# Two of sixteen gate projections computed as seven Strassen products inside the values' stage of a decoder layer, with the other gates dealt out anew

## The chip, the cores and the metric

The kernel runs on one core of a Trainium2 chip. The metric is device time in microseconds (us) for one launch. A version's time is the median of its runs; before the change there are three. Besides these one execution was profiled, and every view of the trace here comes from it.

The engines are named as the profile names them: PE is TensorE (matmuls), PEld its weight loads, DVE is VectorE, ACT is ScalarE, POOL is GpSimd, and SP is SyncE, which here does nothing but start DMAs. Each takes its instructions strictly in order; a wait at the head of an engine's list holds all that stands behind it.

## The reference

One layer, 1024 tokens, model width 1024, all in float32. What matters here is the first projection and where its columns go:

```python
h = rms_norm(x, pre_mix_g[l])
proj = h @ w_in[l]
qa, ka, va, qb, kb, vb, gates = jnp.split(proj, split_at, axis=-1)
...
g_a, g_b = jnp.split(jax.nn.sigmoid(gates), 2, axis=-1)
mix = (g_a * ya + g_b * yb) @ w_mix_out[l]
x = x + rms_norm(mix, post_mix_g[l])
...
y = (jax.nn.gelu(gate, approximate=True) * val) @ w_down[l]
x = x + rms_norm(y, post_ffn_g[l])
```

`ya` comes from a differential attention of four heads (A), `yb` from three groups of four dilated window heads (B), merged by their log-sum-exps. The values `va` and `vb` are together 2048 columns of `proj`, the gates another 2048, which is sixteen tiles of 128 columns.

## The kernel before

**Products.** A float32 product is made of three passes over operands that were split into a rounded high part and a rest: high by high, low by high, high by low (`mm3`, L153 to 157). One product step is therefore three matmuls with a 128x128 stationary and a 128x512 moving operand. A weight tile of 128x512 reaches this form in three moves: SP starts its load into a tile `raw` (`load_raw`, L126), ACT writes the high part `whi` (L149), DVE subtracts to get the low part `wlo` (L146).

**Stages.** The stages follow one another on PE without a gap in the program: the values' stage (up to about 162 us into the span), the four heads of attention A, the twelve heads of attention B, the two output products with the gates (`branch`, from L1178), the mix, then the up and down products of the MLP.

**The values' stage** (L467 to 667) computes the 2048 value columns by Strassen's scheme: halves of the tokens, of the 1024 rows of the weight and of the columns make 2x2 blocks, and seven products `p1` to `p7` replace eight. There are two such sets (`i` = 0 and 1), each product has four steps (`k`), and each step is 12 matmuls into four PSUM banks. `steps_v` lists the 56 steps by hand. All that a step needs is made ahead of it:

- `fetch_v` loads the weight tiles, 8 to 10 steps ahead; `p5` and `p7` need two tiles each. The loads go round robin through six `raw` tiles, and from L646 on also through pieces of tiles of the rotary tables that have served their turn (`more_tags`).
- `ready_v`, up to 5 steps ahead, forms sums of weight tiles on DVE (`wz`, all by the helper `tt` at L345) and splits the result.
- `step_v` runs the matmuls; at a product's last step `take_v` moves the four banks into the result tiles `yv`: some are copied by ACT, some added by DVE. This is traced at a high priority (`tc.high_priority`).
- `put_v` multiplies finished tiles by the norm's factor on DVE (L550) and stores them to the buffer `v_d` in HBM, by DMAs that POOL starts (L551). `STORE_AT` says at which steps this is done for the first set.

Into the same steps are woven the sums of squares of the norm, `angles` and `make_sines` (the rotary tables, L354 to 368 and L425), `turn_norms` (the norm's factors turned by eight PE transposes into a row `rstd_row`, L428 to 435) and `scale_tables` (tables times that row, by L383 and L345, and three stores to `tab_d` by POOL, L444).

**A gate** (`proj_t` with `put_gate`, L234 to 253) is a tile of 128 gate columns by 1024 tokens: two weight loads of 128x512, two splits, 16 product steps (48 matmuls with two halves of tokens), and per half a DVE product with `rstd_row` and a store to `gt_d`, which ACT's queue starts. The gates depend on nothing but `h`, so they serve as filler: `START_GATES` run right behind the values' stage, `A_FILLS` says for each head of attention A which pieces are spread between its blocks (`g` a gate, `p` the next head's projections, `P` the first projection of B, `v` and `x` loads of values, `w` and `V` their splits), and `B_GATES` run in the last head of B. `proj_b` and `split_b` do the same for B's projections and values.

**Order.** A scheduler orders each engine's instructions from the traced program, its priorities, and a model of the engines' timing; only what is marked by `behind_marks` or `issue_after` is tied to a place. The order of a program is fixed when it is built. Where the text speaks of what stands where, it means this fixed order.

Of the kernel before, what the change touches and what calls it, by code (L numbers as in the profile page):

```python
# [43 lines left out]
FULL = 2  # L44


NH = NF // 2
AHEAD, T1_AT, LAST = 4, 5, 7
MIX_UNITS = {3: (0,), 4: (1,), 5: (2, 4), 6: (5,), 7: (6, 3, 7)}
START_GATES, A_FILLS, B_GATES = 1, ("gpgg", "gpvgg", "wgpgg", "xgPVgg"), 3  # L50
SLOTS = 18
LEFT_PAD = 48


XT_BUFS, NORM_AT, ANGLES_AT, SINES_AT, TABLES_AT, STORE_AT = 6, 14, 25, 33, 34, {35: 0, 36: 3, 39: 2, 41: 1}

K_FIRST = (4, 0, 5, 1, 6, 2, 7, 3)
RSQRT_MAGIC = float(0x5F3759DF)
# [29 lines left out]
def trunk(ctx: ExitStack, tc: tile.TileContext, a, out):  # L88
# [372 lines left out]
    with ExitStack() as st_y:  # L461
# [6 lines left out]
        def turns(pattern, *ps):  # L468

            ks = [iter(range(4)) for _ in ps]  # L470
            return [(ps[c], 1, next(ks[c])) for c in pattern]

        steps_v += [("p1", 1, k) for k in range(4)] + turns((0, 0, 1, 0, 1, 0, 1, 1), "p5", "p6")
        steps_v += turns((0, 0, 1, 1, 1, 1, 0, 0), "p3", "p7") + [("p4", 1, k) for k in range(4)]
        wz = [t[:, k % 2] for t in [wv.tile([P, 2, 512], F32, tag=f"wz{i}", name="wz") for i in range(2)] for k in range(2)]
        ready, got_v = {}, {}
# [10 lines left out]
        def new_y(name, pool=None):  # L487
            return [(pool or yv).tile([P, 512], F32, tag=f"y{name}{m}", name="yv") for m in range(4)]

        def fetch_v(n):  # L490
            p, i, k = steps_v[n]
            which = {"p1": ((0, 0),), "p2": ((0, 1),), "p5": ((1, 0), (1, 1)), "p6": ((0, 0),), "p7": ((0, 0), (1, 0)),
                     "p4": ((1, 1),), "p3": ((0, 1),)}[p]
            got_v[n] = [load_raw(a["w_v"][j * 4 + k][:, (2 * i + c) * 512 : (2 * i + c + 1) * 512], next(tags), parts=1 if n else 2)
                        for c, j in which]

        def ready_v(n, w=512):
            p, _, k = steps_v[n]
# [54 lines left out]
        quarter = {(0, i): new_y(f"a{i}") for i in range(2)}  # L553
        banks = {}

        def step_v(n):
            p, i, k = steps_v[n]
            x = xs_of[p]
            if p in ("p1", "p2", "p5") and k == 0:
                left = p == "p1"  # L560
                banks[left] = ([psum() for _ in range(3)] + [psum(F32, ps_o, "o")] if left else
                               [psum(F32, q, t) for q, t in ((ps_s, "s"), (pt, "pt")) for _ in range(2)])
            use = banks[p in ("p1", "p6", "p7", "p4")]
            wh, wl = ready.pop(n)
            for m in range(4):
                tk = slice(m * P, (m + 1) * P)
                mm3(use[m], x[0][:, k, tk], x[1][:, k, tk], wh, wl, k == 0 and p in ("p1", "p2", "p5"), k == 3, p in ("p6", "p7", "p4", "p3"))
            if k < 3:
                return
            with tc.high_priority(offset=80):  # L570
                for m in range(4):
                    take_v(p, i, m, use[m])
            if p == "p7" and i == 0:
                for m in range(4):
                    tt(quarter[3, 0][m], banks[False][m], quarter[3, 0][m], ALU.add)
# [56 lines left out]
        for n in range(8, len(steps_v)):  # L632
            p, i, k = steps_v[n]
            while fetched < min(n + (8 if n <= TABLES_AT else 10), len(steps_v)):
                fetch_v(fetched)
                fetched += 1
            while made < min(n + 5, len(steps_v)):
                ready_v(made)
                made += 1
            if 0 <= n - NORM_AT < 11:  # L640
                norm_x(n - NORM_AT)
            if n == NORM_AT + 11:
                lambda_scale()
            if n == TABLES_AT + 2:
                scale_tables(*args)
            if n == TABLES_AT + 4:  # L646
                tags = more_tags()
            if n == ANGLES_AT:
                pos = [load_raw(a["positions"][sl].partition_broadcast(P), next(tags)) for sl in halves()]
                args = [tb.tile([P, S], F32, tag=n_, name=n_) for n_ in ("sin", "cos")]  # L650
                angles(pos, *args, tb)
            if n in STORE_AT:
                put_v(STORE_AT[n], 0, True)
            if n == SINES_AT:
                make_sines(*args)
            if n == TABLES_AT:
                turn_norms()
            if k == 0 and (p, i) in places_y:
                q, name, pool = places_y[p, i]
                quarter[q, i] = new_y(name, pool)  # L660
            step_v(n)
            if k == 3 and i and p in ("p1", "p7", "p4", "p3"):
                put_v({"p1": 0, "p7": 3, "p4": 2, "p3": 1}[p], 1, p == "p1")
            if (p, i) == ("p5", 1):

                again.append(load_raw(a["xT"][k][:, 512:], next(tags)))
            if (p, i) == ("p6", 1):
                with behind_marks():
                    split_x(k, halves()[1], again[k])
# [18 lines left out]
    def split_values(vs, res):  # L688

        with behind_marks():  # L690
            for v in vs:
                res.append(v_tiles())
                split(*res[-1], v)
# [175 lines left out]
        later(1, sums)  # L869
        later(3, norm)  # L870

    free_gates = list(range(2 * KC))

    def gates(n):

# [6 lines left out]

    tabs_b, wk_b = [], []

    def proj_b(g, h, res, between=None):
        dil = DIL[g]
        qh, ql, kh, kl = (slot(n) for n in ("qh", "ql", "kh", "kl"))
        res += [qh, ql, kh, kl]
        n = 512 // dil

        def put(hi, lo):
            def evacuate(half, sl, ps):
                t = rotated(ps, *tabs_b, sl, 64).rearrange("p (i r) -> p r i", r=dil)
                o, l = (t_.rearrange("p (r i) -> p r i", r=dil)[:, :, half * n : (half + 1) * n] for t_ in (hi, lo))
                nc.scalar.activation(o, t, AF.Copy)
                nc.vector.tensor_tensor(l, t, o.bitcast(F32), op=ALU.subtract)
            return evacuate

        yield from proj_t(QB + g * 512 + h * P, put(qh, ql))
        if between:  # L900
            between()
        yield from proj_t(KB + g * 512 + h * P, put(kh, kl))
# [12 lines left out]
    def fetch_b(pair, g):  # L915
        got_b[pair, g] = fetch_values(DIL[g], 512 + g * 512 + pair * 256)

    def split_b(pair, g):
        split_values(got_b.pop((pair, g)), vs_b[pair, g])

    def a_weight(i):

# [220 lines left out]
    for n, (pair, g, h) in enumerate(steps[:-1]):  # L1143
        sbs = []
        todo = [functools.partial(attend_b, g, h, jj, ops_b[pair, g, h], vs_b[pair, g], sbs) for jj in range(4)]
        nxt = steps[n + 1]
        if h % 2:
            fetch_b(*nxt[:2])
        fill = proj_b(nxt[1], nxt[2], ops_b[nxt], functools.partial(split_b, *nxt[:2]) if h % 2 else None)
        interleave(jobs(todo), 4, (itertools.chain(fill, once(load_ots)) if nxt == steps[-1] else fill, 8))  # L1150
        if pair == 1 and g < 2 and h == 2:
            for i, fn in zip((0, 2, 3, 6, 9), merge(g)):
                later(i, fn, 0)
# [648 lines left out]
```

## Time and profile before

| what | value |
|---|---|
| median of three runs | 1684.5 us (1682.96, 1684.5, 1685.84) |
| the profiled execution's own time | 1684.85 us |
| its span in the trace | 1683.1 us |
| time outside the span | 1.75 us |
| mean granted clock of PE | 0.999 |
| PE busy in the span | 1668.5 us, 99% |
| DVE busy | 1308.4 us, 78% |
| ACT busy | 913.4 us, 54% |
| POOL busy | 170.2 us, 10% |
| DMA | 241.59 MB, mean 144 GB/s |

Busy time counts an instruction from its start to its end; matmuls overlap, so a PE that is 99% busy has hardly a moment in which none runs, and its time is the number of matmuls times the distance of two starts, plus the waits. A row of a timeline gives the start, the duration, the engine, the line, the operation, output and inputs with their shapes, and how many such instructions in a row it sums up; in brackets stands idle time before it and what ended it. Tile names in views of the trace are without buffer numbers.

### The profile page before, as it was taken

How to read it: one execution, taken by the hardware profiler on the slowest of the kernel's cores; microseconds unless marked ns; L12 is line 12 of the kernel's file. 1: busy time of each engine (PE TensorE's matmuls, PEld its weight loads, DVE VectorE, ACT ScalarE, POOL GpSimd, SP SyncE). 2: the span in 40 equal slices, each digit the busy share in tenths (PEclk: the TensorE clock that was granted, in tenths of full speed). 3: DMA queues.
4: the chain of work that ended last, by engine and by line, in shares of the span. 5: the costliest groups of instructions: out<-in, count | busy, mean ns of one | idle time of the engine just before them, and what ended most of it. 6: DMA issues, size and time to landing. Idle time of an engine off the chain costs nothing. (4 is left out here: it accounts for less than half of the span.)

```text
span 1683.1 us, 22937 instructions
## 1 busy us (share of the span) xinstructions
PE 1668.5 (99%) x7878; PEld 1394.0 (83%) x7878; DVE 1308.4 (78%) x2430; ACT 913.4 (54%) x1707; POOL 170.2 (10%) x267
## 2 busy tenths in 40 slices
PE   9999999999999999999999999999999999999997
PEld 7888888888888888888888888887888888888886
DVE  8795576877777777788766865988888778799978
ACT  7633574655445677667554533565554455255453
POOL 0031000000000000000123400022211121000000
PEclk9999999999999999999999999999999999999999
DMA  8767421315122212343676532267755655296524
GB/s 269 234 221 266 132 83 62 107 57 147 48 70 75 76 57 78 107 135 105 212 264 223 188 113 89 58 159 172 161 133 132 156 137 126 96 348 214 193 88 150
DMA packets 117253, 241.59 MB, mean 144 GB/s; under 512 B 14528, under 2 KB 23680, under 8 KB 117136
## 3 DMA queue, kind: packets, MB, share of 16 engines
q1 hardware_dynamic: 89296, 171.28, 30.6%
q0 software_dynamic: 23088, 60.45, 15.2%
q10 hardware_dynamic: 4752, 8.39, 1.3%
q8 instruction: 62, 1.02, 0.3%
q14 instruction: 55, 0.45, 0.1%
HBM read 177.54 MB, written 47.86 MB: 134 GB/s over the span
## 5 line engine op out<-in xcount | busy, mean ns | idle before, releaser
L157 PE MATMUL acc<-xl,whi 128*128 128x512 f32 x768 | 302.5, 394 | 0.0
L155 PE MATMUL acc<-xh,whi 128*128 128x512 f32 x768 | 302.0, 393 | 0.0
L156 PE MATMUL acc<-xh,wlo 128*128 128x512 f32 x768 | 301.7, 393 | 0.0
L149 ACT ACTIVATE whi<-raw 128x512 fp32r<-128x512 f32 (+1 forms) x249 | 154.1, 627 | 180.6 <-PE acc L157 115.4
L146 DVE TENSOR_TENSOR wlo<-raw,whi 128x512 fp32r<-128x512 f32 (+1 forms) x249 | 172.2, 700 | 32.8 <-ACT whi L149 27.9
L156 PEld LDWEIGHTS acc<-xh,wlo 128*128 128x128 f32 x768 | 144.4, 188 | 27.9
L157 PEld LDWEIGHTS acc<-xl,whi 128*128 128x128 f32 x768 | 144.4, 188 | 27.7
L155 PEld LDWEIGHTS acc<-xh,whi 128*128 128x128 f32 x768 | 144.5, 188 | 27.3
L155 PE MATMUL acc<-mh,whi 128*128 128x512 f32 x384 | 149.7, 390 | 1.7 <-ACT u L1447 1.3
L156 PE MATMUL acc<-mh,wlo 128*128 128x512 f32 x384 | 149.4, 389 | 0.0
L157 PE MATMUL acc<-ml,whi 128*128 128x512 f32 x384 | 149.1, 389 | 0.0
L700 ACT ACTIVATE t<-acc 64x512 f32<-64x512 f32 (+1 forms) x160 | 94.7, 592 | 62.0 <-PE acc L157 60.4
L149 ACT ACTIVATE whi<-s 128x512 fp32r<-128x512 f32 x80 | 49.8, 627 | 90.7 <-PE acc L157 63.5
L1443 DVE TENSOR_TENSOR u<-acc,u 128x512 f32<-128x512 f32 x100 | 68.5, 687 | 29.1 <-PE acc L157 28.9
L701 DVE TENSOR_TENSOR t<-acc,cos 128x512 f32<-128x512 f32 x64 | 44.2, 690 | 55.4 <-ACT t L700 51.9
L155 PEld LDWEIGHTS acc<-mh,whi 128*128 128x128 f32 x384 | 72.1, 188 | 17.7 <-ACT u L1447 2.2
L157 PEld LDWEIGHTS acc<-ml,whi 128*128 128x128 f32 x384 | 72.1, 188 | 14.9
L156 PEld LDWEIGHTS acc<-mh,wlo 128*128 128x128 f32 x384 | 72.1, 188 | 14.9
L1620 PE MATMUL acc<-whi,wlo 128*128 128x512 f32 x216 | 76.1, 390 | 0.0
L1619 PE MATMUL acc<-whi 128*128 128x512 f32 x216 | 74.8, 389 | 0.0
L1621 PE MATMUL acc<-wlo,whi 128*128 128x512 f32 x216 | 71.6, 390 | 0.0
L787 DVE CUSTOM_DVE_ANT_0 s<-s,mask_a 128x512 f32<-128x512 f32 (+3 forms) x96 | 52.5, 555 | 23.2 <-PE s L785 18.5
(402 smaller groups left out, 4015.2 us busy)
## 6 DMA issues: line engine op xcount, KB each, us to landing
raw<-in_w_in SPq DMA_DIRECT2D x96, 256.0 KB, 2.8
raw<-in_w_v SPq DMA_DIRECT2D x71, 256.0 KB, 4.6
raw<-in_w_up SPq DMA_DIRECT2D x68, 256.0 KB, 3.6
raw<-c_d SPq DMA_DIRECT2D x48, 256.0 KB, 3.6
c_d<-c SPq DMA_DIRECT2D x22, 512.0 KB, 4.0
s<-in_w_up POOLq DMA_DIRECT2D x40, 256.0 KB, 4.2
s<-s POOLq DMA_DIRECT2D x40, 256.0 KB, 3.9
raw<-in_w_down SPq DMA_DIRECT2D x37, 256.0 KB, 3.5
```

The lines of the kernel that those rows point to most:

```text
L146: eng.tensor_tensor(lo, src, hi.bitcast(F32), op=ALU.subtract)
L149: copy = nc.scalar.activation(hi, src, AF.Copy)
L155: nc.tensor.matmul(o, sh, mh, start=first, stop=False, skip_group_check=on)
L156: nc.tensor.matmul(o, sl, mh, start=False, stop=False, skip_group_check=on)
L157: nc.tensor.matmul(o, sh, ml, start=False, stop=last, skip_group_check=on)
L700: nc.scalar.activation(t1[dst], ps[src], AF.Copy)
L701: nc.vector.tensor_tensor(t2, ps, cos[:, sl], op=ALU.mult)
L787: nc.vector.tensor_tensor_reduce(out=s_sb[:, c0:c1], in0=ps, in1=mask, scale=-scale, scalar=3.0e38, op0=ALU.add, op1=ALU.min, accum_out=mx ...
L1443: nc.vector.tensor_tensor(to, made(p), x, op=ALU.add)
L1619: nc.tensor.matmul(banks[m], gh[:, tk], wh, start=f == 0, stop=False)
L1620: nc.tensor.matmul(banks[m], gl[:, tk], wh, start=False, stop=False)
L1621: nc.tensor.matmul(banks[m], gh[:, tk], wl, start=False, stop=f == NH - 1)
```

## The change

With `PAIRS = 1`, gates 14 and 15 are no longer computed as plain gates. The two form one more Strassen set within the values' stage: two gates by two halves of the tokens by two halves of the rows of the weight. Each of the seven products is one step of 12 matmuls into one PSUM bank. The seven steps stand among those of the second set's `p1` (`steps_v` has 63 now). The gate's weights are taken in the four 128x512 blocks of `w_in`; `fetch_v` loads nine tiles for them, since `p5` and `p7` take two each, and they go through the same `raw` tiles and `wz` sums.

- `step_gate` runs a step. The left bank is one tile of pool `pt` and takes `p1`, then `p6`, `p7` and `p4` on top; the right bank is one tile of `s` and takes `p2`, `p5`, `p3`.
- `take_gate` moves the sums between products: `p2`, `p6` and `p7` are copied by ACT into four `yv` tiles, `p1`, `p7` and `p3` are followed by a DVE addition that reads a bank, and each finished tile is multiplied by `rstd_row` on DVE and stored to `gt_d` by POOL.
- The four `yv` tiles are those which the first set's `p2`/`p1` and `p5`/`p7` results had (names `a0` and `b3`), once these were stored.
- Steps of gates are made ready 4 steps ahead instead of 5; `more_tags` begins four steps later; `STORE_AT` has other steps.

Of the fourteen plain gates none runs at the start now, 2, 3, 3 and 4 run in the four heads of attention A (3 each before), and 2 run in the last head of B (3 before). The loads and splits of values have other places among the fills. In attention B, `split_b` is done in two pieces, ahead of the next head's first projection and between the two, and `fetch_b` comes one head earlier. `NH` keeps its value.

On PE the two gates were 96 matmuls and are 84. Elsewhere the change removes for them 4 loads, 4 ACT splits, 4 DVE subtractions, 4 DVE products and 4 stores from ACT's queue; it adds 9 loads on SP, 7 ACT splits, 3 ACT copies, 7 DVE subtractions, 4 DVE sums of weights, 3 DVE additions, 4 DVE products and 4 stores from POOL.

```diff
-START_GATES, A_FILLS, B_GATES = 1, ("gpgg", "gpvgg", "wgpgg", "xgPVgg"), 3
+PAIRS, START_GATES, A_FILLS, B_GATES = 1, 0, ("gpg", "gpvggw", "gpxggV", "gPggg"), 2
-XT_BUFS, ..., STORE_AT = 6, 14, 25, 33, 34, {35: 0, 36: 3, 39: 2, 41: 1}
+XT_BUFS, ..., STORE_AT = 6, 14, 25, 33, 34, {32: 0, 37: 3, 42: 2, 46: 1}
...
-        steps_v += [("p1", 1, k) for k in range(4)] + turns((0, 0, 1, 0, 1, 0, 1, 1), "p5", "p6")
+        gate_steps = [(p, "gate", 0) for p in ("p2", "p1", "p5", "p6", "p7", "p4", "p3")]
+        own = [("p1", 1, k) for k in range(4)]
+        steps_v += [*own[:2], *gate_steps[:4], own[2], gate_steps[4], own[3], *gate_steps[5:]]
+        steps_v += turns((0, 0, 1, 0, 1, 0, 1, 1), "p5", "p6")
...
+        def take_gate(p, n, use):
+            def put(q):
+                sl = halves()[q % 2]
+                y = gate_y[n][q]
+                tt(y, use if p == "p4" else y, rstd_row[:, sl], ALU.mult)
+                nc.gpsimd.dma_start(gt_d[gate_of(n, q // 2)][:, sl], y)
+            y = gate_y[n]
+            if p in ("p2", "p6", "p7"):
+                nc.scalar.activation(y[{"p2": 0, "p6": 1, "p7": 3}[p]], use, AF.Copy)
+            if p == "p1":
+                tt(y[0], use, y[0], ALU.add)
+                put(0)
+            if p == "p7":
+                tt(y[3], banks[n, False], y[3], ALU.add)
+                put(3)
+            if p == "p4":
+                put(2)
+            if p == "p3":
+                tt(y[1], use, y[1], ALU.add)
+                put(1)
+
+        def step_gate(p, n, wh, wl):
+            left = p in ("p1", "p6", "p7", "p4")
+            if p in ("p1", "p2"):
+                banks[n, left] = psum(F32, pt, "pt") if left else psum(F32, ps_s, "s")
+            x, use = xs_of[p], banks[n, left]
+            for k in range(4):
+                c = slice(k * P, (k + 1) * P)
+                mm3(use, wh[:, c], wl[:, c], x[0][:, k], x[1][:, k], k == 0 and p in ("p1", "p2", "p5"), k == 3, ...)
+            with tc.high_priority(offset=80):
+                take_gate(p, n, use)
...
-            while made < min(n + 5, len(steps_v)):
+            while made < min(n + (4 if i == 'gate' else 5), len(steps_v)):
...
-            if n == TABLES_AT + 4:
+            if n == TABLES_AT + 8:
                 tags = more_tags()
...
+            if (p, i, k) == ("p2", "gate", 0):
+                ya, yb = new_y("a0"), new_y("b3", yw)
+                gate_y.update({x: {0: ya[x], 1: ya[2 + x], 3: yb[x], 2: yb[2 + x]} for x in range(PAIRS)})
...
-    free_gates = list(range(2 * KC))
+    free_gates = list(range(2 * (KC - PAIRS)))
...
-    def split_b(pair, g):
-        split_values(got_b.pop((pair, g)), vs_b[pair, g])
+    def split_b(pair, g, n=2):
+        vs = got_b[pair, g]
+        split_values([vs.pop(0) for _ in range(n)], vs_b[pair, g])
...
-        if h % 2:
-            fetch_b(*nxt[:2])
-        fill = proj_b(nxt[1], nxt[2], ops_b[nxt], functools.partial(split_b, *nxt[:2]) if h % 2 else None)
+        if h % 2 == 0 and n + 2 < len(steps):
+            fetch_b(*steps[n + 2][:2])
+        fill = proj_b(nxt[1], nxt[2], ops_b[nxt], *([functools.partial(split_b, *nxt[:2], 1)] * 2 if h % 2 else ()))
```

More of the change, by code (lines that the diff above doesn't have):

```diff
@@ L44 @@
 FULL = 2
-NH = NF // 2
+NH = (NF + 0) // 2
 AHEAD, T1_AT, LAST = 4, 5, 7
 MIX_UNITS = {3: (0,), 4: (1,), 5: (2, 4), 6: (5,), 7: (6, 3, 7)}
-START_GATES, A_FILLS, B_GATES = 1, ("gpgg", "gpvgg", "wgpgg", "xgPVgg"), 3
+PAIRS, START_GATES, A_FILLS, B_GATES = 1, 0, ("gpg", "gpvggw", "gpxggV", "gPggg"), 2
 SLOTS = 18
 LEFT_PAD = 48
-XT_BUFS, NORM_AT, ANGLES_AT, SINES_AT, TABLES_AT, STORE_AT = 6, 14, 25, 33, 34, {35: 0, 36: 3, 39: 2, 41: 1}
+XT_BUFS, NORM_AT, ANGLES_AT, SINES_AT, TABLES_AT, STORE_AT = 6, 14, 25, 33, 34, {32: 0, 37: 3, 42: 2, 46: 1}
 K_FIRST = (4, 0, 5, 1, 6, 2, 7, 3)
@@ L488, in new_y, with gate_of @@
             return [(pool or yv).tile([P, 512], F32, tag=f"y{name}{m}", name="yv") for m in range(4)]
+        def gate_of(x, c):
+            return 2 * (KC - PAIRS + x) + c
         def fetch_v(n):
@@ L493, in fetch_v @@
                      "p4": ((1, 1),), "p3": ((0, 1),)}[p]
-            got_v[n] = [load_raw(a["w_v"][j * 4 + k][:, (2 * i + c) * 512 : (2 * i + c + 1) * 512], next(tags), parts=1 if n else 2)
-                        for c, j in which]
+            if i == "gate":
+                srcs = [w_in[where[GT + gate_of(k, c) * P]][:, j * 512 : (j + 1) * 512] for c, j in which]
+            else:
+                srcs = [a["w_v"][j * 4 + k][:, (2 * i + c) * 512 : (2 * i + c + 1) * 512] for c, j in which]
+            got_v[n] = [load_raw(src, next(tags), parts=1 if n else 2) for src in srcs]
         def ready_v(n, w=512):
@@ L554, in trunk @@
         banks = {}
+        gate_y = {}
+        def take_gate(p, n, use):
[25 more added lines that the diff above has]
+                c = slice(k * P, (k + 1) * P)
+                mm3(use, wh[:, c], wl[:, c], x[0][:, k], x[1][:, k], k == 0 and p in ("p1", "p2", "p5"), k == 3, p in ("p6", "p7", "p4", "p3"))
+            with tc.high_priority(offset=80):
+                take_gate(p, n, use)
         def step_v(n):
             p, i, k = steps_v[n]
+            if i == "gate":
+                step_gate(p, k, *ready.pop(n))
+                return
             x = xs_of[p]
@@ L883, in trunk, with proj_b @@
     tabs_b, wk_b = [], []
-    def proj_b(g, h, res, between=None):
+    def proj_b(g, h, res, ahead=None, between=None):
         dil = DIL[g]
@@ L897, in put @@
             return evacuate
+        if ahead:
+            ahead()
         yield from proj_t(QB + g * 512 + h * P, put(qh, ql))
```

## The prediction

> **What bounds the kernel now.** I read the busy shares first, then the waits of PE, then the stage that the change touches, slice by slice.
>
> ```profile
> span 1683.1 us, 22937 instructions
> PE 1668.5 (99%) x7878; PEld 1394.0 (83%) x7878; DVE 1308.4 (78%) x2430; ACT 913.4 (54%) x1707; POOL 170.2 (10%) x267
> ```
> ```profile
> PE acc L155 <- ACT xh L387: 1.4, 1, 1.4
> PE acc L155 <- DVE ya L1211: 1.4, 2, 0.9
> PE acc L155 <- ACT u L1447: 1.3, 1, 1.3
> PE pt L594 <- DVE t4l L591: 1.2, 1, 1.2
> PE acc L155 <- ACT mh L149: 0.3, 1, 0.3
> PE acc L156 <- DVE xl L383: 0.2, 1, 0.2
> ```
>
> PE is the bound: all its waits (total, times, longest) come to 5.8 us. Fewer matmuls shorten the span, as long as nothing makes PE wait. In the stage that takes the new products the second engine is not idle either:
>
> ```profile
> 80.00:90.00 10.00, 10.00 (x46) 8.29 (x45) 10.00 (x20) 6.34 (x10) 0.00 (x0) 1.00 0.14 46
> 90.00:100.00 10.00, 10.00 (x46) 8.29 (x45) 10.00 (x20) 2.42 (x4) 0.00 (x0) 1.00 0.79 229
> 100.00:110.00 10.00, 10.00 (x50) 8.38 (x49) 9.67 (x20) 4.12 (x6) 2.66 (x1) 1.00 0.56 190
> 110.00:120.00 10.00, 10.00 (x45) 8.25 (x44) 10.00 (x21) 1.90 (x4) 8.80 (x14) 1.00 0.79 277
> 120.00:130.00 10.00, 10.00 (x45) 8.27 (x45) 9.02 (x16) 5.84 (x10) 5.04 (x9) 1.00 1.03 380
> 130.00:140.00 10.00, 10.00 (x46) 8.26 (x45) 4.67 (x7) 3.58 (x6) 0.00 (x0) 1.00 0.96 334
> ```
>
> The columns are the stretch and its length, then PE, PEld, DVE, ACT and POOL busy, PE's clock, the share of the DMA engines and GB/s. From 80 to 120 us DVE is full (39.67 of 40), and from 120 to 140 the DMA engines are. The seven new steps stand just there. PE does not wait in it before: what DVE does late there, nobody needs soon.
>
> **The saving.** PE's price is the distance of two starts. The second set's first `p1` step begins at 95.55; the matmul at 108.69 is the 58th after it:
>
> ```profile
> 95.55 0.39 PE L155 MATMUL acc<-whi,xh 128*128 128x512 f32 x1
> ...
> 108.69 0.40 PE L156 MATMUL pt<-whi,xl 128*128 128x512 f32 x1
> 108.93 1.04 PE L434 MATMUL s<-ident,rstd_row 128*128 128x128 f32 x8
> 109.72 0.47 PE L157 MATMUL pt<-wlo,xh 128*128 128x512 f32 x1
> ```
>
> So 13.14 / 58 = 0.2266 us each, and the eight transposes 0.79. Two gates take 84 matmuls for 96: 12 x 0.2266 = **2.72 us saved**. That is all there is to gain on PE, and every other edit can only move waits.
>
> **The first new wait: PE at the gate's `p6`.** In DVE's order after the change, this is what stands between the last weight split of the second set's `p1` (`wlo_1205`) and the addition that reads the gate's left bank `pt_1155` with `p1` in it:
>
> ```order
> L146 TENSOR_TENSOR wlo_1205<-raw_1083,whi_1204 128x512
> L146 TENSOR_TENSOR wlo_1232<-raw_1104,whi_1231 128x512
> L383 SCALAR_TENSOR_TENSOR neg_1178<-sin_899,rstd_row_112 128x512
> L345 TENSOR_TENSOR cos_900<-cos_900,rstd_row_112 128x512
> L383 SCALAR_TENSOR_TENSOR neg_1178<-sin_899,rstd_row_112 128x512
> L345 TENSOR_TENSOR cos_900<-cos_900,rstd_row_112 128x512
> L146 TENSOR_TENSOR wlo_1237<-wz_135,whi_1236 128x512
> L345 TENSOR_TENSOR sin_899<-sin_899,rstd_row_112 128x512
> L345 TENSOR_TENSOR yv_141<-acc_1067,yv_141 128x512
> L345 TENSOR_TENSOR yv_142<-acc_1068,yv_142 128x512
> L345 TENSOR_TENSOR yv_143<-acc_1069,yv_143 128x512
> L345 TENSOR_TENSOR yv_1119<-pt_1155,yv_1119 128x512
> ```
>
> Before, the additions for `p1` stood behind the store's products, and the tables came later:
>
> ```order
> L550 TENSOR_SCALAR yv_475<-yv_475,edge_58 128x512
> L550 TENSOR_SCALAR yv_476<-yv_476,edge_58 128x512
> L345 TENSOR_TENSOR yv_141<-acc_1061,yv_141 128x512
> L146 TENSOR_TENSOR wlo_1179<-wz_135,whi_1178 128x512
> L345 TENSOR_TENSOR yv_142<-acc_1062,yv_142 128x512
> L345 TENSOR_TENSOR yv_143<-acc_1063,yv_143 128x512
> ```
>
> What moved: the gate's addition is behind 16 store products instead of 12 and five operations on tables. PE's order there after the change (`pt_1155` and `s_1127` are the gate's banks, `wlo_1205` its own step's weight):
>
> ```order
> L157 MATMUL o_1070<-wlo_1205,xh_98 128x512
> L155 MATMUL s_1127<-xh_98,whi_1055 128x512
> ...
> L155 MATMUL pt_1155<-t2h_116,whi_1086 128x512
> ...
> L155 MATMUL s_1370<-whi_1275,xh_98 128x512
> ...
> L155 MATMUL pt_1155<-t3h_118,whi_1174 128x512
> ...
> L157 MATMUL s_1370<-wlo_1276,xh_98 128x512
> ```
>
> These are the starts of the gate's `p5`, of `p6`, of the next set's `p5`, of the gate's `p7`, and of that next `p5`'s low part. `p6` adds on top of a bank that DVE must first have read. When can each be there? PE: from 95.55 on there stand 84 matmuls and the transposes ahead of `p6`, so 95.55 + 84 x 0.2266 + 0.79 = 115.4. DVE: its order is the same as before up to the first of the two splits at 90.14, and these rows of before give prices and an anchor:
>
> ```profile
> 90.14 1.28 DVE L146 TENSOR_TENSOR wlo<-raw,whi 128x512 fp32r<-128x512 f32 x2
> ...
> 105.85 0.69 DVE L430 COPY rstd_row<-edge 128x1024 f32<-128x1024 f32 x1
> 106.45 4.84 DVE L550 TENSOR_SCALAR yv<-yv,edge 128x512 f32<-128x512 f32 x12
> 111.20 0.69 DVE L345 TENSOR_TENSOR yv<-acc,yv 128x512 f32<-128x512 f32 x1
> 111.81 0.69 DVE L146 TENSOR_TENSOR wlo<-wz,whi 128x512 fp32r<-128x512 f32 x1
> ```
>
> A two-input operation takes 0.60 from start to start (111.81 - 111.20), a store product 4.75 / 12 = 0.396. After the change four two-input operations fewer stand ahead of this place, so it begins at 105.85 - 4 x 0.60 = 103.45. From there to the addition's end are 16 store products (6.33), the copy (0.60), 13 two-input operations (7.8) and the addition itself (0.69): 118.9. The slice from 100 to 110 has 0.33 us of idle DVE that may go, so I take 118.7. PE waits **3.3 us** (a little of it shows at the low part of `wlo_1205` and at `p5`, whose bank ACT clears behind a split that waits for the same DVE row). Bounds: 0 if DVE reached the addition by 115.4, 3.5 with the idle time kept. Before, the same kind of addition ran at 111.20 and nobody missed it.
>
> **Two small waits behind it.** `p6` ends at 118.7 + 2.72 = 121.4. The next set's `whi_1275` needs a `wz` sum four rows behind the addition (118.7 + 2.4 = 121.1) and an ACT split:
>
> ```profile
> 105.45 0.63 ACT L149 ACTIVATE whi<-wz 128x512 fp32r<-128x512 f32 x1 [0.20 <-DVE wz L345]
> ```
>
> So 121.75, 0.3 late. Four matmuls later, at 122.65, the gate's `p7` needs ACT to have copied `p6` out; the copy stands behind a second split: 121.75 + 2 x 0.63 = 123.0, **0.35** late. Bounds: 0 and 1.3 for both. `p7` then ends at 125.7.
>
> **The second new wait: a load that was asked for late.** Next on PE is `wlo_1276`. On DVE it stands behind a sum of two raw tiles:
>
> ```order
> L345 TENSOR_TENSOR yv_1119<-yv_1119,rstd_row_112 128x512
> L559 TENSOR_SCALAR yv_144<-yv_144,edge_58 128x512
> L345 TENSOR_TENSOR wz_136<-raw_1200,raw_1202 128x512
> L146 TENSOR_TENSOR wlo_1276<-wz_135,whi_1275 128x512
> ```
>
> This sum serves a later step; `wlo_1276` only stands behind it. `raw_1202` takes the tile of `raw_1149`, which DVE reads last in the second row behind the gate's addition, so SP can start the load at 118.7 + 1.2 = 119.9 at the earliest. With a time L to land, `wlo_1276` is ready at 119.9 + L + 1.3, and PE wants it at 125.7: a wait of L - 4.5. What L is, three windows of before show (100 to 106, 122.8 to 123.5 and 123.5 to 126 us):
>
> ```profile
> raw<-in_w_v SPq DMA_DIRECT2D x5, 256.0 KB, 4.6
> ```
> ```profile
> raw<-in_w_v SPq DMA_DIRECT2D x1, 256.0 KB, 7.6
> ```
> ```profile
> raw<-in_w_v SPq DMA_DIRECT2D x3, 256.0 KB, 10.4
> ```
>
> and that DVE is then held:
>
> ```profile
> 130.50 0.69 DVE L345 TENSOR_TENSOR raw<-raw 128x512 f32<-128x512 f32 x1 [1.49 <-DMA raw<-in_w_v]
> 134.49 0.69 DVE L345 TENSOR_TENSOR wz<-raw,wz 128x512 f32<-128x512 f32 x1 [3.29 <-DMA raw<-in_w_v]
> ```
>
> The three prices give waits of 0.1, 3.1 and 5.9. The load falls between the quiet window and the crowded one, among 16 stores of values that POOL starts from about 104 on and the first stores of tables. I take the middle of the lower two rows less a little, 5.7 us, since most of the stores are under way earlier than before: **1.2 us**. Both ends stay in the range.
>
> **What I cost at nothing.** DVE's ten and ACT's six additional instructions are in those starts already. ACT's queue loses four stores, POOL gets four behind all others. The start gate is gone: PE then reaches the first head's projections 10.9 us sooner (48 x 0.2266), with three free banks between it and the first need of the tables; a late table would show on DVE first. The fills: no head of A or B has a PE wait in the list above, so smaller ones stay hidden; if that cover is gone it costs part of a gate. The pieces of `split_b` move by a few blocks under the same cover.
>
> **The sum.** -2.72 + 3.3 + 0.3 + 0.35 + 1.2 = +2.4. The profiled execution took 1684.85 (span 1683.1 and 1.75 around it), so 1687.3; the median is 0.35 lower: **1686.95**. A measurement of this kernel can tell about 0.2%, 3.4 us, from no change: 1681.1 to 1687.9 counts as the same.
>
> **The rivals.**
>
> *The gain comes through.* DVE gains 3.3 us somewhere, say by a shorter pitch between its operations: -2.72, 1681.8, which is still "the same". Against it are the slices with 10.00 of 10. Chance 0.12. If the two waits at L1211 (1.4 us) go as well, since fewer gates are ahead of them, it is -4.1, 1680.4: 0.05.
>
> *The late load decides, and it is slower.* Place: the sum of `raw_1200` and `raw_1202`. With L = 7.6 the total is +4.3, 1688.85; with 9.5 +6.2, 1690.75. From L = 6.7 on the result is slower by over 0.2%. For it: DMA shares of 0.96 to 1.03 from 120 on. Against: 0.79 in the slice before. Chance 0.34.
>
> *The clock falls.* The longest pause in the list is 1.4 us, and PE's clock column stands at 1.00 in the slice around it, as everywhere:
>
> ```profile
> 20.00:30.00 10.00, 8.42 (x36) 6.35 (x35) 10.00 (x18) 8.59 (x16) 0.27 (x1) 1.00 0.72 234
> ```
> ```profile
> 5.32 0.99 PE L155 MATMUL s<-whi,xh 128*128 128x512 f32 x1
> 6.10 0.58 PE L156 MATMUL s<-whi,xl 128*128 128x512 f32 x1
> 6.51 0.39 PE L157 MATMUL s<-wlo,xh 128*128 128x512 f32 x1
> 6.75 0.40 PE L155 MATMUL s<-whi,xh 128*128 128x512 f32 x1
> ```
>
> At the program's start a matmul took 0.41 (6.51 - 6.10) instead of 0.23. If a pause of the second wait's upper end, 5.9 us, brought that state back for some fifteen matmuls, 15 x 0.18 = 2.7 us come on top of +7.1: 1694. Chance 0.03. The Trainium skill, "TensorE: Matmul & The Clock Gate", Part 1, says that an idle window of about 3.4 us puts the clock to half until PE has been busy as long; by that rule neither pause of my sum cools PE, and the trace agrees so far as it goes, with 1.4 us at 1.00.
>
> *The last head starves.* It has two gates for three, 10.9 us less to put beside the merge of B; L1211 waits there already (1.4). Half of that as a wait gives +7.8, 1692. Against: DVE and DMA chains there start earlier too. Chance 0.03.
>
> **Chances.** My forecast has 0.43. Faster 0.05; same 0.43 + 0.12 = 0.55; slower 0.34 + 0.03 + 0.03 = 0.40. The range reaches from the case without waits to a load of 9.5 us: 1681.6 to 1690.8; left out are 0.05 below, and 0.06 for the clock, the last head and still later loads each some, together below 0.2.
>
> **What would show it.** Right: among the waits of PE a new one for DVE `yv` at L345 of about 2.5 to 3.3 us near 115.5 to 118.7, and one for DVE `wlo` at L146 near 126, with a DVE wait for `raw<-in_w_v` beside it; 7829 matmuls of the program instead of 7841. Wrong: no PE wait between 110 and 130, or waits of over 2 us beyond 160 us.

## The result: 0.8% slower, and the profile after

| | before | after |
|---|---|---|
| median, six runs each | 1685.36 us (1682.96 to 1690.4) | 1698.85 us (1697.68 to 1701.92) |
| span of the profiled execution | 1683.1 us | 1697.5 us |
| mean granted clock of PE | 0.999 | 0.996 |

The ratio is 1.0083, with a 95% interval of 1.0072 to 1.0093. That is 13.5 us more, outside the forecast's range. The page of after begins like this:

```profile
span 1697.5 us, 22939 instructions
PE 1670.7 (98%) x7866; PEld 1393.6 (82%) x7866; DVE 1315.8 (78%) x2440; ACT 916.8 (54%) x1713; POOL 170.4 (10%) x271
```

The twelve matmuls are gone (7866 for 7878), but PE waits more. These are the waits of PE in after (total, times, longest), to be held against those of before in the prediction:

```profile
PE acc L155 <- DVE ya L1266: 4.0, 2, 2.8
PE acc L155 <- DVE gl L1298: 2.9, 1, 2.9
PE acc L155 <- ACT obh L149: 2.6, 2, 1.6
PE acc L155 <- ACT xh L387: 2.5, 2, 1.3
PE pt L155 <- DVE yv L345: 1.6, 1, 1.6
...
PE s L157 <- DVE wlo L146: 1.2, 1, 1.2
...
PE s L155 <- ACT whi L149: 0.7, 1, 0.7
```

The forecast's waits are the last three. The first three are at the start of `branch`, which multiplies the attentions' outputs (`obh`, `obl`: their split form) by the output weights; 800 us after the new steps. The stretches of 50 us say where the time went (columns as in the prediction). After:

```profile
100.00:150.00 50.00, 46.45 (x206) 37.21 (x205) 43.18 (x79) 18.13 (x31) 16.90 (x27) 1.00 0.89 308
900.00:950.00 50.00, 41.73 (x163) 32.88 (x162) 33.36 (x39) 20.49 (x32) 20.33 (x23) 0.90 0.56 189
```

Before:

```profile
100.00:150.00 50.00, 50.00 (x227) 41.46 (x226) 42.47 (x77) 20.66 (x34) 18.66 (x27) 1.00 0.77 271
900.00:950.00 50.00, 50.00 (x222) 41.43 (x221) 42.44 (x53) 27.46 (x41) 26.55 (x23) 1.00 0.64 210
```

**The values' stage** lost 50 - 46.45 = 3.55 us, and in the places that were forecast. PE's and DVE's timelines of after:

```profile
117.24 0.50 PE L155 MATMUL pt<-t2h,whi 128*128 128x512 f32 x1 [1.64 <-DVE yv L345]
121.00 0.50 PE L155 MATMUL s<-whi,xh 128*128 128x512 f32 x1 [0.72 <-ACT whi L149]
126.19 0.50 PE L157 MATMUL s<-wlo,xh 128*128 128x512 f32 x1 [1.18 <-DVE wlo L146]
```
```profile
116.51 0.67 DVE L345 TENSOR_TENSOR yv<-pt,yv 128x512 f32<-128x512 f32 x1
124.84 0.69 DVE L345 TENSOR_TENSOR wz<-raw 128x512 f32<-128x512 f32 x1 [2.37 <-DMA raw<-in_w_v]
125.45 1.28 DVE L146 TENSOR_TENSOR wlo<-wz,whi 128x512 fp32r<-128x512 f32 x2
```

The gate's `p6` waits for the addition, the next `whi` is a little late, and `wlo` stands behind a sum that waits 2.37 us for its load.

**The start of `branch`** lost 50 - 41.73 = 8.27 us of waits, and the clock fell besides (0.90). PE's timeline of after there:

```profile
887.53 0.28 PE L777 MATMUL o<-pt,vh 128*128 128x256 f32 x1
...
912.68 0.79 PE L155 MATMUL acc<-obh,whi 128*128 128x512 f32 x1 [2.77 <-DVE ya L1266]
914.55 0.79 PE L155 MATMUL acc<-obh,whi 128*128 128x512 f32 x1 [1.07 <-ACT obh L149]
915.14 0.63 PE L156 MATMUL acc<-obh,wlo 128*128 128x512 f32 x1
...
918.98 0.53 PE L157 MATMUL acc<-obl,whi 128*128 128x512 f32 x1
...
925.16 0.50 PE L155 MATMUL acc<-obh,whi 128*128 128x512 f32 x1 [1.57 <-ACT obh L149]
...
929.68 0.80 PE L155 MATMUL acc<-obh,whi 128*128 128x512 f32 x1 [2.86 <-DVE gl L1298]
930.27 0.63 PE L156 MATMUL acc<-obh,wlo 128*128 128x512 f32 x1
...
932.83 0.44 PE L156 MATMUL acc<-obh,wlo 128*128 128x512 f32 x1
```

The first row begins the last value product of attention B (four matmuls). From it a chain runs that has little of PE in it: the head's output is added up (`osb`), stored, loaded again, merged with the other groups (`mw`), and split into `obh` and `obl`, for each half of the tokens. Only other matmuls can cover it. In before that product began earlier:

```profile
873.53 0.28 PE L725 MATMUL o<-pt,vh 128*128 128x256 f32 x1
```

Counted in the timelines, 109 matmuls of `branch` for A stand behind it in before, and no wait. In after 52 are left, then 35 of `branch` for B up to the first long pause, as halves of `obh` arrive.

**The account.** Waits 3.55 and 8.27; nine distances from 915.14 to 918.98 and six from 930.27 to 932.83 of 0.427 each in place of 0.2266, 15 x 0.200 = 3.0; seven pauses (three and four), each with 0.16 more, since a matmul of 0.39 ends with none overlapping it (0.39 - 0.2266), and 0.11, since the first distance behind it is 0.34, together 1.9; the matmuls on both sides of those slow runs, which were slow themselves (0.79 and 0.80 in the rows at 912.68, 914.55 and 929.68, and the two that end the runs), another 1.1. The longer wait for `xh` near the start, 2.5 for 1.4, costs nothing: the same matmul stands at 28.71 in after and at 28.91 before, 0.2 sooner. The waits for `u` and the other one for `ya` are 0.6 less. Less 2.72 for the matmuls the sum is +14.3, measured +14.4.

### The profile page after: what moved, and what is told of

Its sections match the earlier page's. It is cut to its first block, busy times and chain, and to the rows that moved or that the text cites. A ratio compares the mean times of both kernels' runs of the same rounds, so it can differ in the third digit from the quotient of the medians.

```text
span 1697.5 us, 22939 instructions
## 1 busy us (share of the span) xinstructions
PE 1670.7 (98%) x7866; PEld 1393.6 (82%) x7866; DVE 1315.8 (78%) x2440; ACT 916.8 (54%) x1713; POOL 170.4 (10%) x271
## 3 DMA queue, kind: packets, MB, share of 16 engines
q0 software_dynamic: 23408, 61.50, 15.4%
## 5 line engine op out<-in xcount | busy, mean ns | idle before, releaser
L155 PE MATMUL acc<-xh,whi 128*128 128x512 f32 x736 | 289.3, 393 | 0.3 <-DVE t L753 0.3
L156 PE MATMUL acc<-xh,wlo 128*128 128x512 f32 x736 | 289.6, 393 | 0.0
L157 PE MATMUL acc<-xl,whi 128*128 128x512 f32 x736 | 289.2, 393 | 0.0
L155 PEld LDWEIGHTS acc<-xh,whi 128*128 128x128 f32 x736 | 138.4, 188 | 27.2 <-DVE t L753 0.7
L156 PEld LDWEIGHTS acc<-xh,wlo 128*128 128x128 f32 x736 | 138.3, 188 | 26.8
L157 PEld LDWEIGHTS acc<-xl,whi 128*128 128x128 f32 x736 | 138.4, 188 | 26.6
L846 ACT ACTIVATE s<-s,mx 128x896 f32<-128x896 f32 (+7 forms) x64 | 49.3, 771 | 32.4 <-DVE mx L839 17.4
```

Of the source, the lines that this page charges most:

```text
L155: nc.tensor.matmul(o, sh, mh, start=first, stop=False, skip_group_check=on)
L156: nc.tensor.matmul(o, sl, mh, start=False, stop=False, skip_group_check=on)
L157: nc.tensor.matmul(o, sh, ml, start=False, stop=last, skip_group_check=on)
L846: exp = nc.scalar.activation(sc[c][:, :w], sc[c][:, :w], AF.Exp, bias=mx[:, c, 0:1], scale=-1.0, accum_out=den[:, c : c + 1])
```

## The experiments

Two theories for the large part. **Merge**: the chain behind the last head got longer, by the two-piece split of B's values or by two gates for three in the last head. **Reserve**: the gates beside the attentions are one common stock of filler. The scheduler spends it where it is wanted, and what runs short shows up where the deal is thinnest. Before has 12 + 3 = 15 such gates, after 12 + 2 = 14, since one of the two Strassen gates was a start gate and the other a filler. For the small part: DVE's order (tables and store products ahead of the addition), or the load asked for late.

The "loss" of a place below is what the distances of successive matmul starts there have beyond the usual one for their shape, summed from the timeline: 4.7 us in the values' stage of after, 13.4 at the start of `branch`.

### Where the fillers stand

**e1**, after with the moved gate back in B:

```diff
-PAIRS, START_GATES, A_FILLS, B_GATES = 1, 0, ("gpg", "gpvggw", "gpxggV", "gPggg"), 2
+PAIRS, START_GATES, A_FILLS, B_GATES = 1, 0, ("gpg", "gpvggw", "gpxggV", "gPgg"), 3
```

> The changed kernel with one gate moved from the last head of attention A to the last head of B (fills 2, 3, 3, 3 and 3 there). In PE's order 147 matmuls of branch a then stand behind the last value product of B instead of 52. Theory (the merge of the last head is no longer covered by work behind it, and each wait there cools PE): the pauses and the slow clock after 890 us go, 13 us of the 14; what stays is the values' stage, -2.7 + 4.0: 1685 to 1688 us. Rival (the stage of the values, its stores or its waits cause the late pauses too): 1695 or more.

1692.88 us, ratio 1.0047 (1.0032 to 1.0062). The start of `branch` was whole again (loss 1.1), but the time missed its forecast: a loss of 6.8 us appeared in the first head of B, where neither before nor after had one. A window of e1 and PE's timeline there:

```profile
560.00:570.00 10.00, 6.48 (x35) 5.33 (x34) 9.20 (x20) 9.33 (x23) 0.00 (x0) 0.76 0.02 4
```
```profile
564.62 0.73 PE L777 MATMUL o<-pt,vh 128*128 128x512 f32 x3 [1.87 <-DVE osb L1083]
567.79 0.79 PE L155 MATMUL acc<-xh,whi 128*128 128x512 f32 x1 [1.65 <-DVE t L753]
```

DVE and ACT are at 9.2 and 9.3 of 10 there, the DMA share is 0.02: PE waits for what these two engines do in the head, and for no load. The hole had moved 340 us ahead.

**e2**, before with the changed deal, and so without the Strassen gates (two gates at the start, 14 beside the attentions):

```diff
-START_GATES, A_FILLS, B_GATES = 1, ("gpgg", "gpvgg", "wgpgg", "xgPVgg"), 3
+START_GATES, A_FILLS, B_GATES = 2, ("gpg", "gpvggw", "gpxggV", "gPggg"), 2
```

> The kernel before, all sixteen gates plain and the values' stage untouched, with gates dealt out as in the change: 2 at the start, 2, 3, 3, 4 in the heads of A, 2 in the last head of B. 58 matmuls of branch a behind the last value product, 109 before. Theory (cover): pauses after 890 us and slow clock as in the changed kernel, 9 to 13 us: 1694 to 1699 us. Rival (Strassen stage): no change, 1684 to 1687.

1692.58 us, 1.0039 (1.0024 to 1.0054), with a loss of 8.3 at the start of `branch` and none in the values' stage; a little under the expected range. The deal alone, without a Strassen gate, makes half of the slowdown, 6.7 of 13.5 us. At the start of `branch` it makes 8.3 of the 13.4 that after lost there; why the same deal costs 5 us more with the Strassen gates no run separates.

**e3**, before with two gates in the last head of B and four in the last of A: 15 again.

```diff
+START_GATES, A_FILLS, B_GATES = 1, ("gpgg", "gpvgg", "wgpgg", "xgPVggg"), 2
```

> The kernel before with one gate moved from the last head of B to the last head of A: fills 1 at the start, 3, 3, 3, 4 in A and 2 in B. The scheduler here sets the last head's blocks early: 124 matmuls of branch a behind the last value product. Theory (cover behind the last value product, not the number of gates): no new pauses, 1683 to 1687 us. Rival (one gate fewer in the last head of B is what starves it): pauses as in the changed kernel, 1692 to 1699.

1687.53 us, 1.0008 (0.9999 to 1.0018): the same as before. Its windows at the start of `branch`:

```profile
910.00:920.00 10.00, 9.29 (x41) 7.28 (x40) 7.82 (x13) 7.16 (x10) 0.70 (x1) 1.00 0.78 283
920.00:930.00 10.00, 10.00 (x45) 8.28 (x45) 8.75 (x11) 6.78 (x11) 7.98 (x6) 1.00 0.41 131
```

The last head has the same two gates as in after, and 124 matmuls of `branch` for A stand behind its last value product. A wait of 2.03 us for `ya` at 876 is left, and the time is not clear of that of before. So two gates in the last head aren't the cause, and **merge** falls in that form.

**e4**, after with the values of B split whole and fetched as before, and **e5**, e1 with the same:

```diff
-        if h % 2 == 0 and n + 2 < len(steps):
-            fetch_b(*steps[n + 2][:2])
-        fill = proj_b(..., *([functools.partial(split_b, *nxt[:2], 1)] * 2 if h % 2 else ()))
+        if h % 2:
+            fetch_b(*nxt[:2])
+        fill = proj_b(..., None, functools.partial(split_b, *nxt[:2]) if h % 2 else None)
```

> The changed kernel with attention B's loads and splits of values as before: both pieces at once, between the two projections, and the loads a head later. 58 matmuls of branch a behind the last value product instead of 52. Theory (cover): the pauses stay, at most 1.5 us less: 1696 to 1699 us. Rival (the split in two pieces delays the last heads): 1685 to 1690.

> The changed kernel with three gates in the last head of B (and three in the last of A), and B's splits whole: in PE's order the last head then reads as in the kernel before (109 matmuls of branch a behind the last value product). Theory (cover for the late pauses, two pieces of the split for the pauses of the first run at 564 us): both go; what stays is the values' stage, 2.72 saved and 4 to 6.5 us of waits: 1686 to 1690 us with the kernel before at about 1685.9. Rival (the new dealing of fills costs elsewhere as well): 1691 or more.

e4: 1697.18 us, 1.007 (1.0047 to 1.0092), with a loss of 8.1 at the start of `branch` and 5.8 just ahead of it, in a profiled execution that took 1701.34. e5: 1694.04, 1.0058 (1.0045 to 1.0071), with a loss of 6.5 in the first head of B. The pieces of the split neither cause the holes nor cure them.

**e9**, e5 with before's fills less one `g`, and **e12**, before with the loads and splits of values moved as in after, but 15 gates:

```diff
 e9
+PAIRS, START_GATES, A_FILLS, B_GATES = 1, 0, ("gpg", "gpvgg", "wgpgg", "xgPVgg"), 3
 e12
+START_GATES, A_FILLS, B_GATES = 1, ("gpgg", "gpvggw", "gpxggV", "gPgg"), 3
```

> The change's values' stage with the fills of the kernel before but for one gate: 0 at the start, 2, 3, 3, 3 in A with the loads and splits of B's values in the last head of A again, 3 in the last head of B, splits whole. Theory (the 6.5 us near 575 us in the runs with three gates in the last head of A come from the loads and splits having left that head): they go, the late pauses too; left are -2.7 and 4.7 to 7 us of the values' stage: 1686.5 to 1689.5 us with the kernel before at 1685. Rival (the two Strassen gates shift everything): the 6.5 us stay, 1693.

> The kernel before, all gates plain, 1 at the start, 3 in each head of A and 3 in the last of B as before, but the loads and splits of values where the change has them (a head earlier). Theory (that move makes the pauses near 575 us): 5 to 7 us slower at 560 to 585 us, 1690 to 1692 with the kernel before at 1685. Rival (only with Strassen gates): 1684 to 1686.

e9: 1695.48, 1.0059 (1.0047 to 1.0072), a loss of 6.0 in the first head of B, against my expectation. e12: 1686.84, 1.0013 (1.0004 to 1.0022), and no loss there. Where the `w`, `v`, `x` and `V` stand is not it; the missing gate is what was left.

### The count itself

Before, with nothing changed but how many of its sixteen plain gates run at the start:

```diff
 e13 (14 beside the attentions)
+START_GATES, A_FILLS, B_GATES = 2, ("gpg", "gpvgg", "wgpgg", "xgPVgg"), 3
 e14 (13)
+START_GATES, A_FILLS, B_GATES = 3, ("gpg", "gpvg", "wgpgg", "xgPVgg"), 3
 e15 (16)
+START_GATES, A_FILLS, B_GATES = 0, ("gpgg", "gpvgg", "wgpggg", "xgPVgg"), 3
```

> The kernel before, all gates plain and the values' stage untouched, with one gate moved from the first head of A to the start: 2 at the start, 2, 3, 3, 3 in A and 3 in the last of B, so 14 gates are left beside the attentions instead of 15. PE's order then has 8.0 us of the first heads of B without any filler, as the Strassen runs with three gates at the end have. Theory (14 gates are one too few for filler, wherever they come from): 5 to 7 us of pauses and slow clock near 560 to 590 us, 1690 to 1692 with the kernel before at 1685. Rival (the pauses belong to the Strassen gates): 1684 to 1686.5.

> As the run before in this list with another gate moved to the start: 3 there, 2, 2, 3, 3 in A, 3 in B, 13 beside the attentions. In PE's order no stretch of over 4 us is without filler here. If a common reserve of filler runs dry (one reading of the theory): slower than the run before by up to another gate, 1692 to 1700. If only the stretch without filler in the order costs (the other reading): back to 1685 to 1688.

> The kernel before without a gate at the start, 16 beside the attentions (3, 3, 4, 3 in A, 3 in B). Theory (filler): no pauses beyond those of the kernel before, 1683 to 1686; rival (the start gate hides the tables' loads): a wait for a table after 165 us, 1 to 5 us slower.

| beside the attentions | median | ratio (95%) | loss |
|---|---|---|---|
| 16 (e15) | 1685.98 us | 0.9995 (0.9985 to 1.0005) | 1.3, values' stage |
| 15 (before) | 1685.88 | | none |
| 14 (e13) | 1690.55 | 1.0032 (1.0022 to 1.0043) | 5.4, first head of B |
| 13 (e14) | 1698.99 | 1.0075 (1.0057 to 1.0093) | 9.2, a head of A; 4.3, first head of B |

The matmuls are the same in all four. One window of e13 and PE's rows in it:

```profile
570.00:580.00 10.00, 6.68 (x49) 5.64 (x47) 8.30 (x18) 9.21 (x23) 0.00 (x0) 1.00 0.14 54
```
```profile
573.25 0.74 PE L725 MATMUL o<-pt,vh 128*128 128x512 f32 x3 [1.26 <-DVE osb L1028]
...
576.96 0.33 PE L155 MATMUL s<-kh,qh 128*128 128x128 f32 x1 [1.76 <-ACT kh L895]
```

It is a hole in the same head as e1's, again with waits for DVE and ACT, in a kernel without a Strassen gate. e14's new hole, by a window and PE's timeline:

```profile
390.00:400.00 10.00, 5.99 (x20) 4.89 (x20) 9.58 (x29) 3.92 (x8) 1.43 (x3) 0.70 0.66 159
```
```profile
394.83 0.48 PE L784 MATMUL s<-k,a 128*128 128x128 f32 x1 [3.09 <-DVE mx L787]
```

**Reserve** holds in these deals: 15 are just enough, the sixteenth buys nothing, the first one less costs 5 and the next 8 more. Before stood at the edge, and no wait of its profile said so. All the kernels above with 14, of either kind, have such a hole, in the first head of B or at the start of `branch`; e3 and e12, with 15, lose 2.1 us at most in either place.

**e16** gives e10 (below) its fifteenth filler: gate 0 is computed twice, so this kernel has 48 matmuls of useless work, 48 x 0.2266 = 10.9 us.

```diff
-... = 1, 0, ("gpg", "gpvgg", "wgpgg", "xgPVgg"), 3
+... = 1, 0, ("gpgg", "gpvgg", "wgpgg", "xgPVgg"), 3
-    free_gates = list(range(2 * (KC - PAIRS)))
+    free_gates = [0] + list(range(2 * (KC - PAIRS)))
```

> The run with fills as before and the gate's addition ahead of the tables (1692.0), with one plain gate computed twice as pure filler: 3, 3, 3, 3 in A and 3 in B, 15 beside the attentions. It adds 48 matmuls, 10.9 us, that the result doesn't need. Theory: the 6 us near 575 us go, so 10.9 - 6 = 4.9 slower: 1695 to 1698 us. Rival (the pauses there have another cause): they stay, 1702 to 1704.

1701.04 us, 1.0089 (1.007 to 1.0107). The first head of B is whole:

```profile
570.00:580.00 10.00, 10.00 (x53) 8.54 (x52) 7.80 (x15) 7.87 (x15) 0.00 (x0) 1.00 0.09 27
580.00:590.00 10.00, 10.00 (x56) 8.65 (x56) 8.84 (x21) 7.79 (x17) 0.00 (x0) 1.00 0.48 150
```

But the time is 3 us above what I expected. Two other waits came up in it, in the values' stage and late in attention B, by PE's timeline:

```profile
118.76 0.50 PE L155 MATMUL s<-whi,xh 128*128 128x512 f32 x1 [1.87 <-ACT whi L149]
```
```profile
865.86 0.38 PE L778 MATMUL o<-pt,vh 128*128 128x256 f32 x1 [1.98 <-DVE osb L1084]
...
867.42 0.63 PE L157 MATMUL acc<-xl,whi 128*128 128x512 f32 x1
...
869.98 0.63 PE L157 MATMUL acc<-xl,whi 128*128 128x512 f32 x1
```

Behind both, seven distances were 0.42. The place of the hole agrees with **reserve**; the price of a filler within a Strassen kernel was not met, and I have no experiment on why. So no run here shows the Strassen gates with enough filler and no other wait.

### The values' stage

**e7** is e5 with the work on the tables tied behind the addition that `p6` waits for; **e10** is the same tie in e9.

```diff
...
+                gate_add.append(nc.vector.tensor_tensor(y[0], use, y[0], op=ALU.add).ins)
...
-                scale_tables(*args)
+                with tc.issue_after(gate_add[0]):
+                    scale_tables(*args)
```

> As the first run of this list, with one tie of order: the products of the rotary tables come behind the gate's addition that reads p1's bank. All work is kept. Theory (order on a full DVE): the addition ends some 2.4 us sooner, the wait at p6 goes, and the next set's low weight part stands ahead of the sum that waits for the late load: 2 to 5 us below the first run. Rival (the wait only moves to the next load): within 1 us of it.

> As the run before in this list, with the rotary tables' products tied behind the gate's addition that reads p1's bank. With the same tie the values' stage lost 3.2 us instead of 6.9 in an earlier run: 1684 to 1686.5 us, the best of the versions with Strassen gates so far. Rival (a tie that helps only by chance): as the run before, within 1 us.

e7: 1690.48 us, 1.0036 (1.0023 to 1.0048), 3.6 below e5 as expected; its loss in the stage is 3.2 for 6.9, and PE no longer waits at `p6`, but 1.77 for the `whi` that now stands ahead of it. e10: 1692.03, 1.0043 (1.0031 to 1.0056), 3.45 below e9 and still above the 1684 to 1686.5 that I expected, since the hole in the first head of B stayed (loss 6.0). In the stage it lost 4.7 for e9's 5.9, which shows no gain: with one and the same order of PE and DVE up to there the stage lost 4.7 in after, 5.9 in e1 and e9, 6.6 in e4 and 6.9 in e5, from execution to execution. Only e7's 3.2 lies outside these. So the tie gained twice in the median, and that DVE's order has a price of its own in the stage rests on e7. e7 is the fastest of the kernels with Strassen gates, and still slower than before.

**e6** is e5 with the first set's values stored unscaled, so 16 products of DVE are left out. **e8** is e7 with two of the four stores of values tied behind the addition as well.

```diff
 e6
-                if scale:
+                if scale and i:
 e8
+                with tc.issue_after(gate_add[0]) if gate_add and STORE_AT[n] in (1, 2) else nullcontext():
                     put_v(STORE_AT[n], 0, True)
```

> As the run before in this list, but the sixteen DVE products of the first value set with the norm's factor (put_v) are left out, so those values are stored unscaled: 16 x 0.396 = 6.3 us less on DVE ahead of the gate's first addition, stores and loads as they were. Theory (a full DVE makes the waits of the values' stage, directly and by letting go of raw tiles late): waits of PE between 100 and 130 us fall from 4 to 6 us to under 1.5, total 3 to 5 us below the run before. Rival (the DMA engines' late loads make them): within 1 us of the run before.

> As the run before in this list, and the last eight store products of the first set stand behind the same addition, so that raw tiles come free 3 us sooner. Theory: no PE wait over 0.5 us from 100 to 130; 2.7 us saved and nothing given back: 1682.5 to 1684.5 us with the kernel before at 1685.9. Rival (later stores push the loads behind them): a wait for a weight of 1 us or more after 120 us, 1685 or more.

e6: 1695.88, 1.0064 (1.005 to 1.0077). e8: 1695.83, 1.0066 (1.0053 to 1.0079). Both missed. With less work or a stricter tie the addition came no sooner (it began 1.8 us later than in e5, and 2.0 later than in e7), since in the new order a sum of two raw tiles stood ahead of it. DVE's timeline of e8:

```profile
117.53 0.69 DVE L345 TENSOR_TENSOR wz<-raw 128x512 f32<-128x512 f32 x1 [4.41 <-DMA raw<-in_w_v]
...
119.53 0.68 DVE L579 TENSOR_TENSOR yv<-pt,yv 128x512 f32<-128x512 f32 x1
```

In e6 that sum waited 2.98 us. So these runs say that a late load can take the addition's place as the last, not whether DVE was too full.

**e11** is e10 with two more tiles for raw weights, so that loads can start earlier:

```diff
...
+                for tag in ("raw", "t1", "t2", "raw", "t1", "t2"):
+                    yield tag
+                for k in range(2):
+                    yield wv.tile([P, 512], F32, tag=f"rx{k}", name="raw")
...
```

> As the run before in this list, with eight raw tiles for weight loads instead of six in the values' stage, so that loads start some two tiles sooner. Theory (late loads hold DVE, and DVE then the bank and the weights): PE's waits from 100 to 130 us under 1.5 us, 1682.5 to 1684.5 us with the kernel before at 1685. Rival (DVE's order alone): no shorter than the run before.

1695.08, 1.0062 (1.0049 to 1.0075): not shorter. The loss is again 4.7, with a new wait of 1.92 us for `whi` at 105 and one of 1.3 at 63. The order changed with the tiles here too. How much of the stage's loss is the loads' and how much the order's stays open.

## Why the prediction was wrong, point by point

**The saving** was right: twelve matmuls fewer at 0.2266.

**The first new wait** was at the place and for the reason given, and half as long: 1.64 for 3.3. PE came to `p6` at 117.24 - 1.64 = 115.6 (forecast 115.4); DVE ended the addition at 117.18 (forecast 118.7). All the operations that I counted stand there in the trace, and from the first store product to the addition's end they took 117.18 - 101.68 = 15.5 (forecast 15.4). What was off is where they began. DVE's timeline of after, with the splits that stood at 90.14 before, and the first store products:

```profile
88.74 1.28 DVE L146 TENSOR_TENSOR wlo<-raw,whi 128x512 fp32r<-128x512 f32 x2
...
101.68 1.67 DVE L559 TENSOR_SCALAR yv<-yv,edge 128x512 f32<-128x512 f32 x4
```

The anchor came 1.4 us sooner: in the same order of work DVE was busy for 64.20 of the first 80 us, and for 62.93 before. That was luck: in e1 and e5, with the same order of PE and DVE in the stage, the addition ended at 118.20 and 118.69, PE waited 2.37 and 2.40, and the stage lost 5.9 and 6.9 us. The **two small waits** came to one of 0.72 for `whi`, for 0.65 (none showed at `p7`), the **late load** to 1.18 for 1.2. Together 3.55 for 5.15, and 0.8 for what the three pauses cost beside the wait. So in this execution the stage alone would have given -2.72 + 3.55 + 0.8 = +1.6, "the same" as forecast; with the losses of e1 and e5 it is +3.2 to +4.2, at the edge of that.

**What I cost at nothing** is the step that failed: "The fills: no head of A or B has a PE wait in the list above, so smaller ones stay hidden; if that cover is gone it costs part of a gate." The list of waits says that there is no hole; it does not say how much filler is left over. e13 and e14 put the answer at none: the first gate taken away cost 1690.55 - 1685.88 = 4.7 us and the next 8.4. In after the loss at the start of `branch` was 13.4, more than the 10.9 of a whole gate, where I had "part of a gate".

**The last head starves** was the rival that came true in place and sign, with a chance of 0.03 and a price of 7.8. Its reason was half wrong: not the two gates in that head (e3 has them and is not clearly slower), but one gate fewer in all, under a deal that left the shortage at the end. "DVE and DMA chains there start earlier too", held against it, was the wrong way round: the last value product began 14 us later (887.53 for 873.53), with 57 fewer matmuls of `branch` behind it.

**The clock falls** came true as well, but on a far shorter pause than the 5.9 us that I made its condition (next section but one).

**What would show it** worked: "waits of over 2 us beyond 160 us" was named as the sign of a wrong prediction, and 2.77 and 2.86 us stood there. The trace counts 37 matmuls more in both kernels than the prediction's 7829 and 7841; the difference of twelve is as said.

## What to carry to other kernels

A profile without waits shows that the filler was enough, not that any is spare: when a change takes work out of a pool that a scheduler spends freely, measure the pool's edge first, by moving one piece of it out of reach and nothing else. Count the pool as a whole; the hole opens where the deal is thinnest, hundreds of microseconds from the edit, and moves when one place is mended. A saving on the engine that bounds the kernel is worth nothing if the saved work was also the cover for another engine's chain.

## What the runs showed of the hardware that was not expected

PE's clock gave way after pauses of 1.8 to 3 us. In after, 2.77 us and, one matmul later, 1.07 us were followed by nine distances of 0.427, four microseconds; 2.86 us by six. In e9 a single pause of 2.39 us was enough, and the slow rate set in 1.5 us after it. PE's timeline of e9:

```profile
118.89 0.50 PE L155 MATMUL pt<-t2h,whi 128*128 128x512 f32 x1 [2.39 <-DVE yv L345]
...
120.44 0.63 PE L155 MATMUL pt<-t2h,whi 128*128 128x512 f32 x1
120.86 0.63 PE L156 MATMUL pt<-t2h,wlo 128*128 128x512 f32 x1
...
122.57 0.63 PE L157 MATMUL pt<-t2l,whi 128*128 128x512 f32 x1
```

Where the matmuls are all of this shape, six to nine distances of 0.427 for 0.2266 add 1.2 to 1.8 us to the price of such a pause. For a single pause the limit isn't sharp: pauses of 1.87 and 1.98 us in e16 and one of 1.77 in e9 (at 580.59) brought the slow rate, one of 1.92 us in e11 and one of 2.03 in e3 did not (the distances behind them stay at 0.23), nor did the 1.64 us in after. The granted clock says more. Windows of after, then of e9, with borders where it changes:

```profile
912.44:919.27 6.83, 5.52 (x12) 4.04 (x13) 2.08 (x4) 0.63 (x1) 3.72 (x7) 0.50 0.96 307
919.27:929.51 10.24, 5.98 (x25) 4.28 (x24) 7.42 (x10) 4.51 (x8) 0.00 (x0) 1.00 0.74 266
929.51:932.92 3.41, 3.24 (x8) 2.57 (x9) 3.41 (x6) 2.08 (x4) 3.21 (x3) 0.50 0.78 237
```
```profile
116.90:120.31 3.41, 1.43 (x6) 1.21 (x7) 2.58 (x6) 0.00 (x0) 1.08 (x2) 1.00 1.02 401
120.31:123.72 3.41, 3.41 (x10) 2.46 (x9) 3.41 (x7) 1.53 (x3) 1.97 (x4) 0.50 1.00 385
```

It is halved for 3.41 us or twice that, on borders that are whole multiples of 3.41 us apart, wherever PE resumes. The stretch of 3.41 us ahead of e9's slow one had PE busy for 1.43, so idle for 1.98. Laid on that grid, over all traces here that have a slow stretch between 30 and 1600 us, each stretch with 1.87 us idle or more was followed by a slow one, none with 1.62 or less was unless it was slow itself, and between 1.64 and 1.77 both occur. What counts is thus about half of a stretch idle, not one pause's length; a pause that lies across a border is shared by two stretches, which would fit e3 and e11. The Trainium skill, "TensorE: Matmul & The Clock Gate", Part 1, has the half rate after an idle window of about 3.4 us, in windows that run freely. The length and the fixed grid agree with it; that a whole window must be idle does not, since no pause here was as long. The measurement decides.
